# Where half of the MLP's sums of x are made, and by which queue the turned squares travel

## The chip, the cores and the metric

The kernel runs on one core of a Trainium2 chip. The core has a matrix engine (TensorE, PE in the profile, with a second row PEld for loading its stationary operand), a vector engine (VectorE, DVE), a scalar engine (ScalarE, ACT), GpSimd (POOL) and an engine that only issues transfers (SyncE, SP). ACT can issue transfers too; the profile names the queues SPq and ACTq. The metric is the device time of one execution in microseconds.

## The reference

Two residual layers on a sequence of 256 tokens of 2048 features, all in float32. Each layer is a token mixer (stick-breaking attention in the first layer, selected sparse attention in the second) and an MLP:

```python
for i in range(DEPTH):
    h = rms_norm(x, norm_mix[i])
    x = x + mixer(h)                      # ends in o @ w_out
    h = rms_norm(x, norm_mlp[i])
    x = x + jnp.square(jax.nn.relu(h @ w_up[i])) @ w_down[i]
```

`w_up` is 2048 x 8192 and `w_down` 8192 x 2048, so the MLPs hold most of the work.

## The kernel before

**Precision in two parts.** Every product is made from float32 values split into a high part (a copy rounded to the matrix engine's format) and a low part (the value minus the high part). `high` makes `wh` of a weight tile on ACT, `low` makes `wl` on DVE; `xT` holds both parts of the transposed, normalized x. Three products (high by high, high by low, low by high) make one.

**Items.** The whole program is one list of items. An item loads one weight tile of 128 x 1024 (512 KB) and multiplies it; it is given 2.72 us, half that for an item of the seven products below. The main loop at the end goes through the list: for item i it writes `low(i + LEAD)` (LEAD is 3), then `loads`, then `high(i + LEAD + 1)`, perhaps the seeds of an accumulator six items ahead (`before`), then the matmuls of item i and then its `post` functions. `loads` issues, on SP, every weight load for which a buffer is free, for items up to `RAW + 3` = 8 past the one whose `wl` was just written. The tags of the buffers are `wraw` (5) and `sraw` (7 for loads, 2 spare).

**Order.** A scheduler orders each engine's instructions by a timing of its own; what it writes is fixed at build time. `keep_in_program_order` ties an instruction behind the one that was written just before it on the same engine; it can't be put ahead of that one, while others may pass it.

**Sections.** Four sections follow each other: mixer A, MLP, mixer B, MLP. A mixer ends in `out_proj`: 32 items in groups of eight, one group per 512 columns of x, with `add_residual` and `prep` (scaling, transposes, `xT`) behind each group. Each section's `begin` opens a pool of SBUF that is closed when the next section starts.

**The MLP.** The 8192 hidden features are worked through in eight parts f = 0 to 7 of 1024. For f = 0 the product `h @ w_up` is made directly (`up`, 16 items). For f = 1 to 7 (`seven`; a *block* below) it is made by seven products in place of eight quarter products: x is cut in two halves of tokens and two halves of features, and DVE sums quarters of the weights and of x. The sums of x, made once per MLP, are `xS`; `forms` returns its 16 steps, eight for each half b of the feature tiles: two `whole`, four `mixed` and two `parted` (each two copies on ACT and two subtractions on DVE). The steps use scratch in the slot of the second hidden tile `hS` (`draft`) and are made during the `up` items, two at a time (`put(ds, 5, ...)`).

The seven products leave the squared hidden values with tokens on partitions, and the down product wants features there. So at the end of a block come, each at a time after the block's end given by `LAPS` (n = 0 by `LAG` = 2.7 us later than n = 1): `squared` (ACT: relu, square), `turned` (DVE transposes 32 x 32 blocks), `away` (two DMAs to DRAM), `back` (four DMAs from DRAM that finish the transpose) and `parted_h` (high part on ACT, low part on DVE, into `hS`). The DMAs of `away` and `back` are issued by ACT. `back` and the squares take `sraw` slots (`temp`). The last block is turned on PE instead (`turn`).

The items of a block are mixed with 16 items of the down product (`down`: four groups of four items per f), which belong to the part before: `SPAN` says how many go beside the first half of the products, between, and beside the second half; blocks that it does not name take (9, 2, 5). `EARLY` = 5 items of `up` are kept back as the first of these fillers. What is left over follows the last block. A down group ends in `down_done`: two ACT copies of the accumulators to `xs`; the next group is opened by two ACT copies in `seeded`.

Of the kernel before, what the change touches and what calls it, by code (L numbers as in the profile page):

```python
# [8 lines left out]
F32 = mybir.dt.float32  # L9
F32R = mybir.dt.float32r  # L10
# [6 lines left out]
P = 128  # L17
D = 2048
S = 256
# [26 lines left out]
PINNED = 16  # L46
HK = KT // 2
LASTF = 7
SPAN = {1: (7, 2, 5), 2: (8, 2, 5)}
EARLY = 5  # L50
TURNS = (8.0, 10.8)
LAPS = (6.8, 11.5, 18.0, 31.0)
LAG = 2.7
SEED = 6
RAWS = {"wraw": RAW, "sraw": 7}
# [26 lines left out]
def trunk(ctx, tc, x, norm_mix, w_in_a, w_out_a, w_in_b, w_out_b, q_norm_b, k_norm_b, rel_bias,  # L82
# [9 lines left out]
    auxp = ctx.enter_context(tc.tile_pool(name="auxp", bufs=2, space=PSUM))  # L92
    drp = ctx.enter_context(tc.tile_pool(name="drp", bufs=1, space=bass.MemoryType.DRAM))

    opening = tc.tile_pool(name="opening", bufs=1, reuse_waits="tile")
    early = opening.__enter__()

# [103 lines left out]
        dve.tensor_copy(wide["RS"], ps[:, :S])  # L201


    accs = {}

    def rows(w, r0, nr, c0, ncol):
        return w[r0:r0 + nr, c0:c0 + ncol].rearrange("(a p) c -> p a c", p=P)
# [77 lines left out]
    def mlp(l, next_col):  # L285
# [16 lines left out]
        def temp():  # L302
            return sec["pool"].tile([P, WT], F32, name="sraw", bufs=RAWS["sraw"] + SPARE)

        def draft(n):
            if "draft" not in sec:
                sec["draft"] = sec["pool"].tile([P, 4, WT], F32, name="hS", bufs=2)
            return sec["draft"][:, n, :]

        def whole(b, half):  # L310

            t = sec["a", half] = draft(half).rearrange("p (k t) -> p k t", k=4)
            ks = slice(HK * half + 4 * b, HK * half + 4 * b + 4)
            dve.tensor_add(t, xT[:, ks, 0, :].bitcast(F32), xT[:, ks, 1, :].bitcast(F32))

        def mixed(b, n):

            a11, a21 = sec["a", 0][:, :, :P], sec["a", 0][:, :, P:]
            a12, a22 = sec["a", 1][:, :, :P], sec["a", 1][:, :, P:]
            if n % 2 == 0:  # L320
                sec["d", n // 2] = draft(2 + n // 2).rearrange("p (n k t) -> p n k t", n=2, k=4)
            d = lambda m: sec["d", m // 2][:, m % 2]
            if n == 0:
                dve.tensor_sub(d(0), a21, a22)
            elif n == 1:
                dve.tensor_sub(d(1), d(0), a11)
            elif n == 2:
                dve.tensor_sub(d(2), a11, a21)
            else:
                dve.tensor_add(d(3), a12, d(1))  # L330
# [26 lines left out]

        def h_tile(f):
            if f not in sec:
                sec[f] = sec["pool"].tile([P, HK, 2, S], F32R, name="hS", bufs=2)  # L360
            return sec[f]

        def up():
# [6 lines left out]
        def seven(f, c0):  # L370

            g, w = {}, w_up[l]
            quarter = lambda k, t: lambda kt, part: xT[:, HK * k + kt, part, t * P:(t + 1) * P]
            summed = lambda n: lambda kt, part: sec["xS"][:, n, kt, part, :]

            def block(k, n, s, tag):
                return Raw(rows(w, 1024 * k + 256 * s, 256, c0 + 512 * n, 512), KB, 512, tag)

            def item(raws, bank, x, s, source, opens=True):
                def mm(wh, wl):  # L380
# [57 lines left out]
            def se(n):  # L438
                if "se" not in g:
                    g["se"] = sec["pool"].tile([P, 3, 512], F32, name="se", bufs=1)  # L440
                return g["se"][:, n, :]
# [23 lines left out]
            def squared(n):  # L465

                c0, c1 = (se(2), se(1)) if n else (se(0), g["s2"])
                if n:
                    act.activation(c0, c0, AF.Relu)
                act.activation(c1, c1, AF.Relu)  # L470
                for t, c in enumerate((c0, c1)):
                    o = c if f == LASTF else g["sq", n][:, t].rearrange("p (q k b) -> p q b k", q=4, k=4)
                    i = c if f == LASTF else c.rearrange("p (q b k) -> p q b k", q=4, k=4)
                    act.activation(o, i, AF.Square)

            def turn(n, c0, c1):
                h, kts = h_tile(f), slice(4 * n, 4 * n + 4)
                acc = accp.tile([P, 2, 512], F32, name="acc")
                ps = acc.rearrange("p a (k t) -> p (a k) t", k=2)
                for k in range(4):  # L480
                    for t, c in enumerate((c0, c1)):
                        pe.matmul(ps[:, k, t * P:(t + 1) * P], c[:, k * P:(k + 1) * P], ident,
                                  start=k % 2 == 0 and t == 0, stop=k % 2 == 1 and t == 1, is_transpose=True,
                                  skip_group_check=True)
                hi = h[:, kts, 0, :]
                copy(hi, ps)
                dve.tensor_sub(h[:, kts, 1, :], ps, hi.bitcast(F32))
# [10 lines left out]
            def away(n):  # L498
                hd = g["hd", n] = drp.tile([2, P, 512], F32, name="hd", bufs=4)
                for t, c in enumerate((se(2), se(1)) if n else (se(0), g["s2"])):  # L500
                    tc.keep_in_program_order(nc.scalar.dma_start(hd[t], c))

            def back(n):
                hd = g["hd", n].rearrange("t (i b) (q c) -> q b (t i) c", b=32, q=4)
                g["raw", n] = temp().rearrange("p (t c) -> p t c", t=2)
                to = g["raw", n].rearrange("p t (i c) -> p (t i) c", i=4)
                for q in range(4):
                    tc.keep_in_program_order(nc.scalar.dma_start(to[32 * q:32 * q + 32], hd[q]))  # L508

            def parted_h(n):  # L510
                raw = g["raw", n].rearrange("p t (i k a) -> p k (t i) a", i=4, k=4)
# [2 lines left out]
                tc.keep_in_program_order(act.activation(hi, raw, AF.Copy))  # L514
                tc.keep_in_program_order(dve.tensor_sub(lo, raw, hi.bitcast(F32)))

            ends = [(0, after), (1.4, after2), (1.4, lambda: squared(1)), (2.8, lambda: squared(0))]
            if f == LASTF:
                ends += [(TURNS[0], lambda: turn(1, se(2), se(1))), (TURNS[1], lambda: turn(0, se(0), g["s2"]))]
            else:  # L520
                ends.append((0, homes))
                for n in (1, 0):
                    steps = (lambda n=n: turned(n), lambda n=n: away(n), lambda n=n: back(n), lambda n=n: parted_h(n))
                    ends += [(us + (0 if n else LAG), step) for us, step in zip(LAPS, steps)]
                ends.sort(key=lambda e: e[0])
# [50 lines left out]
        def put(items, at, fs, step=1):  # L576
            for n, f in enumerate(fs):
                items[at + n * step].post.append(f)
# [1 line left out]
        ds = up()  # L580
        ds[2 * QA + 1].post.append(stats)
        todo = forms()
        put(ds, 5, [lambda n=n: (todo[2 * n](), todo[2 * n + 1]()) for n in range(8)])
        for f in range(LASTF + 1):
            ds += down(f)
        items, late = ds[:16 - EARLY], []
# [12 lines left out]
        for n, ends in late:  # L599
            at = 0  # L600
            for us, f in ends:
                while at < us:
                    n, at = n + 1, at + items[n + 1].us
                items[n].post.append(f)
        return items, begin


    def mixer_a():
# [3 lines left out]
        def begin(pl):  # L612
            st["pool"] = pl
            st["vs"] = pl.tile([P, 2, D], F32, name="vs", bufs=1)
            st["oT"] = pl.tile([P, HEADS, 2, S], F32R, name="oT", bufs=1)
            st["RSq"] = pl.tile([P, S], F32, name="RSq", bufs=1)
            wide["RS"] = pl.tile([P, S], F32, name="RS", bufs=1)

# [123 lines left out]
    def mixer_b():  # L742
# [3 lines left out]
        def mk(shape, name, dt=F32, bufs=1):  # L746
            return st["pool"].tile(shape, dt, name=name, bufs=bufs)

        def begin(pl):
            st["pool"] = pl  # L750
            st["oT"] = mk([P, HEADS, 2, S], "oT", F32R)
            st["qiT"] = mk([P, 8, S], "w8")
            st["kiT"] = mk([P, S], "kiT")
            wide["RS"] = mk([P, S], "RS")
            st["wi"] = tmp.tile([P, 2, HEADS], F32, name="wi", bufs=1)
            st["sc"] = mk([P, 384], "sc")
            st["mask"] = mk([P, 384], "mask")
            st["kT"] = mk([P, KV, S], "kT")
            st["vh"] = mk([P, 2, 512], "vh", F32R)
            st["vl"] = mk([P, 2, 512], "vl", F32R)  # L760
# [215 lines left out]

    sections = [mixer_a(), mlp(0, 16), mixer_b(), mlp(1, None)]
    items = [it for sec in sections for it in sec[0]]
    first = {}
    n = 0  # L980
    for its, begin in sections:
        first[n] = begin
        n += len(its)
    parts = {}
    queue = []
    for i, it in enumerate(items):
# [68 lines left out]
        if i == 1:  # L1055
            prep(0, 0, False, (1,))
    high(LEAD)
    section, now = None, []
    for i, it in enumerate(items):
        if i in first:  # L1060
            if section is not None:
                section.__exit__(None, None, None)
                if opening is not None:
                    opening.__exit__(None, None, None)
                    opening = None
            section = tc.tile_pool(name=f"section{i}", bufs=1, reuse_waits="tile")
            now[:] = [section.__enter__()]
            first[i](now[0])
        pinned[0] = i < PINNED
        low(i + LEAD)  # L1070
        loads(i + LEAD)
        high(i + LEAD + 1)
        if i + SEED < len(items) and items[i + SEED].before:
            items[i + SEED].before()
        it.mm(*parts.pop(i))
        for f in it.post:
            f()
    section.__exit__(None, None, None)


_INS = ["x", "norm_mix", "w_in_a", "w_out_a", "w_in_b", "w_out_b", "q_norm_b", "k_norm_b", "rel_bias",
# [24 lines left out]
```

## Time and profile before

| | |
|---|---|
| median of 3 runs | 2088.77 us (2087.46, 2095.05, 2088.77) |
| profiled execution | 2094.76 us, of which its span 2093.0 us |
| granted PE clock, mean | 0.994 |
| PE, DVE, ACT busy | 98%, 79%, 65% of the span |
| DMA | 424.05 MB, mean 203 GB/s |
| issued by SP for the weights | 738 loads, nearly all of 512 KB |
| issued by ACT for the squares | 48 `away` of 256 KB, 96 `back` of 128 KB |

The span runs from the first to the last instruction; shares are averages over stages with different limits. Line numbers (L508) are those of the kernel; many operations go through helpers, so that line 107 is every copy on ACT and line 1033 every `wl`. A wait names the engine and line that waited and what it says ended the wait.

### The profile page before, as it was taken

The page shows a single profiled execution, that of the slowest core. Times are in us where ns is not written, and L with a number is a line of the kernel's source. Part 1 is how long each engine was busy: PE and PEld are TensorE (multiplying, and loading weights), DVE is VectorE, ACT ScalarE, POOL GpSimd, SP SyncE. Part 2 cuts the span into 40 slices and gives each one's busy share as a digit, 9 for nine tenths or more (in the row PEclk, how much of TensorE's full clock was granted, in tenths as well). Part 3 has the DMA queues.
Part 4 walks back from the last instruction along what each step waited for, and adds up shares of the span by engine and source line. Part 5 has one row for each costly group of instructions (what it writes and reads, how often), then busy time and mean ns, then how long its engine had stood idle before and what let it go on. Part 6 is the DMA issues. An engine that isn't in the chain of part 4 may idle for free.

```text
span 2093.0 us, 26629 instructions
## 1 busy us (share of the span) xinstructions
PE 2047.4 (98%) x9572; PEld 1700.5 (81%) x9572; DVE 1649.5 (79%) x1745; ACT 1362.6 (65%) x1812; POOL 34.0 (2%) x71
## 2 busy tenths in 40 slices
PE   8999999999899999999999999999989999999999
PEld 7888888887788787787888788888778878778887
DVE  5456665798899998999665877769889999998974
ACT  6445555577677776777764555666767777677774
POOL 0101110000000000000000000000000000000000
PEclk9999999999999999999999999999999999999999
DMA  7666645665766858768566565456575876866844
GB/s 253 193 193 191 176 165 178 192 216 186 235 202 219 252 195 254 210 206 248 163 199 189 157 196 168 151 182 204 185 238 196 250 231 211 258 202 204 260 155 140
DMA packets 274425, 424.05 MB, mean 203 GB/s; under 512 B 16882, under 2 KB 107636, under 8 KB 274292
## 3 DMA queue, kind: packets, MB, share of 16 engines
q1 hardware_dynamic: 233508, 389.74, 58.0%
q10 hardware_dynamic: 40784, 32.61, 5.6%
q8 instruction: 75, 1.23, 0.2%
q14 instruction: 58, 0.48, 0.1%
HBM read 404.41 MB, written 17.82 MB: 202 GB/s over the span
## 4 chain that ended last, share of the span: by engine, by line
PE 88%; DMA 6%; DVE 2%; ACT 2%; issue 1%; ACTq 1%; DVEq 0%; SPq 0%
PE acc L229 47%; PE acc L252 15%; PE acc L387 13%; PE aux L387 9%; DMA sraw<-hd 4%; ACT wh L107 2%; DVE wl L1033 1%; DMA hd<-se 1%; DMA sraw<-in_w_up_dram 1%; PE aux L163 1%; PE aux L229 1%; PE aux L901 1%; DVE sraw L418 0%; ACTq L508 0%; PE acc L637 0%
## 5 line engine op out<-in xcount | busy, mean ns | idle before, releaser
L1033 DVE TENSOR_TENSOR wl<-wraw,wh 128x1024 fp32r<-128x1024 f32 x626 | 756.8, 1219 | 291.0 <-PE acc L229 144.2
L107 ACT ACTIVATE wh<-wraw 128x1024 fp32r<-128x1024 f32 x626 | 650.7, 1057 | 318.5 <-PE acc L229 157.1
L229 PE MATMUL acc<-wh,hS 128*128 128x512 f32 x2016 | 512.2, 392 | 17.6 <-ACT wh L107 14.9
L229 PEld LDWEIGHTS acc<-wh,hS 128*128 128x128 f32 x2016 | 378.5, 189 | 101.0 <-ACT wh L107 19.3
L1033 DVE TENSOR_TENSOR wl<-sraw,wh 128x1024 fp32r<-128x1024 f32 x280 | 337.0, 1219 | 56.0 <-ACT wh L107 41.7
L107 ACT ACTIVATE wh<-sraw 128x1024 fp32r<-128x1024 f32 x280 | 290.4, 1056 | 133.3 <-DVE sraw L425 78.0
L229 PE MATMUL acc<-wl,hS 128*128 128x512 f32 x1008 | 270.2, 389 | 0.0
L252 PE MATMUL acc<-xT,wh 128*128 128x512 f32 x896 | 228.0, 393 | 0.0
L229 PEld LDWEIGHTS acc<-wl,hS 128*128 128x128 f32 x1008 | 189.2, 188 | 39.3
L252 PEld LDWEIGHTS acc<-xT,wh 128*128 128x128 f32 x896 | 160.6, 189 | 28.6 <-ACT wh L107 0.4
L229 PE MATMUL acc<-wh,xT 128*128 128x512 f32 x640 | 165.3, 397 | 0.5 <-ACT wh L107 0.5
L229 PEld LDWEIGHTS acc<-wh,xT 128*128 128x128 f32 x640 | 119.8, 190 | 27.6 <-issue 2.3
L229 PE MATMUL acc<-wh,oT 128*128 128x512 f32 x512 | 133.1, 395 | 0.0
L387 PE MATMUL aux<-wh,xS 128*128 128x512 f32 x448 | 122.2, 394 | 9.7 <-ACT wh L107 9.7
L252 PEld LDWEIGHTS acc<-xT,wl 128*128 128x128 f32 x896 | 123.3, 190 | 9.1
L252 PE MATMUL acc<-xT,wl 128*128 128x256 f32 x896 | 128.6, 283 | 0.0
L387 PE MATMUL acc<-wh,xS 128*128 128x512 f32 x448 | 124.5, 396 | 2.1 <-ACT wh L107 2.1
L107 ACT ACTIVATE xs<-acc 128x512 f32<-128x512 f32 x112 | 60.6, 594 | 97.3 <-PE acc L229 88.7
L387 PE MATMUL acc<-wh,xT 128*128 128x512 f32 x448 | 119.9, 389 | 0.0
L229 PEld LDWEIGHTS acc<-wh,oT 128*128 128x128 f32 x512 | 94.7, 188 | 18.9
L387 PEld LDWEIGHTS aux<-wh,xS 128*128 128x128 f32 x448 | 84.6, 190 | 28.1 <-ACT wh L107 10.9
L387 PEld LDWEIGHTS acc<-wh,xS 128*128 128x128 f32 x448 | 85.8, 193 | 22.3 <-ACT wh L107 4.1
(204 smaller groups left out, 2209.4 us busy)
## 6 DMA issues: line engine op xcount, KB each, us to landing
wraw<-in_w_down_dram SPq DMA_DIRECT2D x256, 512.0 KB, 4.7
sraw<-in_w_up_dram SPq DMA_DIRECT2D x168, 512.0 KB, 5.1
wraw<-in_w_in_a_dram SPq DMA_DIRECT2D x96, 512.0 KB, 3.7
wraw<-in_w_up_dram SPq DMA_DIRECT2D x88, 512.0 KB, 4.4
wraw<-in_w_in_b_dram SPq DMA_DIRECT2D x64, 512.0 KB, 3.7
wraw<-in_w_out_a_dram SPq DMA_DIRECT2D x32, 512.0 KB, 3.5
wraw<-in_w_out_b_dram SPq DMA_DIRECT2D x32, 512.0 KB, 3.9
sraw<-hd ACTq DMA_DIRECT2D x96, 128.0 KB, 7.4
```

What stands on the lines that cost most here:

```text
L107: pin(act.activation(o, i, AF.Copy, scale=scale))
L163: pin(pe.transpose(ps[:, j, t * P:(t + 1) * P], block[t][:, ks], ident))
L229: pin(pe.matmul(acc[t], lhs(k, part, slice(t * P, (t + 1) * P)), w[:, j, :], start=not seed and w is wh and part == 0 and k == 0, stop=w i ...
L252: pe.matmul(acc[:, m, cs], w[:, j, m * P:(m + 1) * P], xT[:, k, xs_, :], start=w is wh and k == 0, stop=w is wl and k == KT - 1)
L387: pe.matmul(acc, x(k, part), w[:, j, :], start=opens and w is wh and part == 0 and k == 0, stop=w is wl and k == HK - 1, **on)
L901: pe.matmul(ps[:, h - lo, :], qT[:, h, t * P:(t + 1) * P], kT[:, n, 0:w], start=True, stop=True)
L1033: pin(dve.tensor_sub(wl, raw, wh.bitcast(F32)))
```

## The change

The change does three things.

1. **Sums.** The two feature halves of x are cut differently (tiles 0 to 3 and 8 to 11 against 4 to 7 and 12 to 15, instead of 0 to 7 against 8 to 15), so that the steps of b = 0 need only the first 1024 columns of x. These eight steps are written behind the last eight items of the preceding output projection, one each; the eight of b = 1 behind `up` items 4 to 11, one each. The scratch comes from `sraw` slots. For this the MLP's pool is opened 13 items into the output projection (`SWAP`), and the attention output `oT` and the hidden tiles `hS` move to a second pool on the right side of SBUF that changes at the old boundary, beside a pad of 120 floats.
2. **Queue.** `away` and `back` are issued by SP.
3. **Times.** `squared` and the homes of its results come later, `LAPS` goes from (6.8, 11.5, 18.0, 31.0) to (9.0, 13.0, 20.0, 29.0), and block 1 gets 15 fillers instead of 14, block 2 16 instead of 15.

```diff
-SPAN = {1: (7, 2, 5), 2: (8, 2, 5)}
+SPAN = {1: (8, 2, 5)}
+SWAP = 13
-LAPS = (6.8, 11.5, 18.0, 31.0)
+LAPS = (9.0, 13.0, 20.0, 29.0)
...
+    edge = ctx.enter_context(tc.tile_pool(name="edge", bufs=1, side="right"))
+    edge.tile([P, 120], F32, name="edge")
...
-            t = sec["a", half] = draft(half).rearrange("p (k t) -> p k t", k=4)
-            ks = slice(HK * half + 4 * b, HK * half + 4 * b + 4)
+            t = sec["a", half] = temp().rearrange("p (k t) -> p k t", k=4)
+            ks = slice(8 * b + 4 * half, 8 * b + 4 * half + 4)
...
-                sec["d", n // 2] = draft(2 + n // 2).rearrange("p (n k t) -> p n k t", n=2, k=4)
+                sec["d", n // 2] = temp().rearrange("p (n k t) -> p n k t", n=2, k=4)
...
-                sec[f] = sec["pool"].tile([P, HK, 2, S], F32R, name="hS", bufs=2)
+                sec[f] = right[0].tile([P, HK, 2, S], F32R, name="hS", bufs=2)
...
-            quarter = lambda k, t: lambda kt, part: xT[:, HK * k + kt, part, t * P:(t + 1) * P]
+            quarter = lambda k, t: lambda kt, part: xT[:, kt // 4 * 8 + 4 * k + kt % 4, part, t * P:(t + 1) * P]
...
-                return Raw(rows(w, 1024 * k + 256 * s, 256, c0 + 512 * n, 512), KB, 512, tag)
+                return Raw(rows(w, 1024 * (s // 2) + 512 * k + 256 * (s % 2), 256, c0 + 512 * n, 512), KB, 512, tag)
...
-                    tc.keep_in_program_order(nc.scalar.dma_start(hd[t], c))
+                    tc.keep_in_program_order(nc.sync.dma_start(hd[t], c))
...
-                    tc.keep_in_program_order(nc.scalar.dma_start(to[32 * q:32 * q + 32], hd[q]))
+                    tc.keep_in_program_order(nc.sync.dma_start(to[32 * q:32 * q + 32], hd[q]))
...
-            ends = [(0, after), (1.4, after2), (1.4, lambda: squared(1)), (2.8, lambda: squared(0))]
+            ends = [(0, after), (1.4, after2)]
             if f == LASTF:
-                ends += [(TURNS[0], lambda: turn(1, se(2), se(1))), (TURNS[1], lambda: turn(0, se(0), g["s2"]))]
+                ends += [(1.4, lambda: squared(1)), (2.8, lambda: squared(0)),
+                         (TURNS[0], lambda: turn(1, se(2), se(1))), (TURNS[1], lambda: turn(0, se(0), g["s2"]))]
             else:
-                ends.append((0, homes))
+                ends += [(3.5, homes), (3.5, lambda: squared(1)), (6.0, lambda: squared(0))]
...
-        put(ds, 5, [lambda n=n: (todo[2 * n](), todo[2 * n + 1]()) for n in range(8)])
+        put(ds, 4, todo[8:])
...
-            st["oT"] = pl.tile([P, HEADS, 2, S], F32R, name="oT", bufs=1)
+            st["oT"] = right[0].tile([P, HEADS, 2, S], F32R, name="oT", bufs=1)
...
+    left, other = {0: sections[0][1]}, {0: None}
     n = 0
-    for its, begin in sections:
-        first[n] = begin
-        n += len(its)
+    for sec, after in zip(sections, sections[1:]):
+        n += len(sec[0])
+        other[n] = None
+        if len(after) == 2:
+            left[n] = after[1]
+            continue
+        wo = n - 4 * QB
+        left[wo + SWAP] = after[1]
+        for k, f in enumerate(after[2]):
+            items[n - len(after[2]) + k].post.append(f)
```

In the main loop the pool on the right side is closed and opened again where an index is in `other`, and the section's pool where it is in `left`.

More of the change, by code (lines that the diff above doesn't have):

```diff
@@ L201, in row_scale_wide @@
         dve.tensor_copy(wide["RS"], ps[:, :S])
-    accs = {}
+    accs, now, right = {}, [], []
     def rows(w, r0, nr, c0, ncol):
@@ L303, in temp @@
             return sec["pool"].tile([P, WT], F32, name="sraw", bufs=RAWS["sraw"] + SPARE)
[L305 to L308, printed above, removed]
         def whole(b, half):
-            t = sec["a", half] = draft(half).rearrange("p (k t) -> p k t", k=4)
-            ks = slice(HK * half + 4 * b, HK * half + 4 * b + 4)
+            t = sec["a", half] = temp().rearrange("p (k t) -> p k t", k=4)
+            ks = slice(8 * b + 4 * half, 8 * b + 4 * half + 4)
             dve.tensor_add(t, xT[:, ks, 0, :].bitcast(F32), xT[:, ks, 1, :].bitcast(F32))
@@ L604, in mlp @@
                 items[n].post.append(f)
-        return items, begin
+        return items, begin, todo[:8]
     def mixer_a():
@@ L750, in begin @@
             st["pool"] = pl
-            st["oT"] = mk([P, HEADS, 2, S], "oT", F32R)
+            st["oT"] = right[0].tile([P, HEADS, 2, S], F32R, name="oT", bufs=1)
             st["qiT"] = mk([P, 8, S], "w8")
@@ L978, in trunk @@
     items = [it for sec in sections for it in sec[0]]
-    first = {}
+    left, other = {0: sections[0][1]}, {0: None}
     n = 0
-    for its, begin in sections:
-        first[n] = begin
-        n += len(its)
+    for sec, after in zip(sections, sections[1:]):
[8 more added lines that the diff above has]
+            items[n - len(after[2]) + k].post.append(f)
     parts = {}
@@ L1057, in trunk @@
     high(LEAD)
-    section, now = None, []
+    section, side = None, None
     for i, it in enumerate(items):
-        if i in first:
+        if i in other:
+            if side is not None:
+                side.__exit__(None, None, None)
+            side = tc.tile_pool(name=f"side{i}", bufs=1, reuse_waits="tile", side="right")
+            right[:] = [side.__enter__()]
+        if i in left:
             if section is not None:
@@ L1067, in trunk @@
             now[:] = [section.__enter__()]
-            first[i](now[0])
+            left[i](now[0])
         pinned[0] = i < PINNED
@@ L1078, in trunk @@
     section.__exit__(None, None, None)
+    side.__exit__(None, None, None)
 _INS = ["x", "norm_mix", "w_in_a", "w_out_a", "w_in_b", "w_out_b", "q_norm_b", "k_norm_b", "rel_bias",
```

## The prediction

> **What bounds the kernel now.** I read the page's busy times first, then TensorE's waits, then the timeline at three of the waits, then the stage table.
>
> ```profile
> span 2093.0 us, 26629 instructions
> ...
> PE 2047.4 (98%) x9572; PEld 1700.5 (81%) x9572; DVE 1649.5 (79%) x1745; ACT 1362.6 (65%) x1812; POOL 34.0 (2%) x71
> ```
>
> PE, the matmuls, is busy for 98% of the span. The change takes no matmul away, so all that it can win is PE's waiting and what that costs in clock. The wait view of PE (total us, count, longest):
>
> ```profile
> PE acc L229 <- ACT wh L107: 15.4, 9, 2.4
> PE aux L387 <- ACT wh L107: 9.7, 2, 4.9
> PE aux L387 <- ACT aux L107: 4.4, 1, 4.4
> ...
> PE acc L229 <- ACT hS L107: 1.9, 1, 1.9
> ```
>
> and the first kind again, in the first 400 us alone:
>
> ```profile
> PE acc L229 <- ACT wh L107: 0.5, 1, 0.5
> ```
>
> So 14.9 us in eight waits of the first kind lie in the MLPs. The timeline says where each kind comes from. Its columns: start, length, engine, line, operation, tiles, count, [idle time before, who ended it]. First ScalarE (ACT) alone, then PE:
>
> ```profile
> 709.57 3.45 ACTq L508 DMA_DIRECT2D sraw<-hd  x3
> 713.07 1.06 ACT L107 ACTIVATE wh<-wraw 128x1024 fp32r<-128x1024 f32 x1 [2.87 <-DMA sraw<-hd]
> ```
> ```profile
> 714.18 2.11 PE L229 MATMUL acc<-wh,hS 128*128 128x512 f32 x8 [2.43 <-ACT wh L107]
> ```
>
> **Issue waits**: ACT stands in three DMA issues of `back` (L508) for 3.45 us, the last of which goes out only when earlier squares have landed. The copy behind them, a `wh` of a weight, needs nothing of those DMAs but is late, and PE waits 2.43 us. I take all eight waits for this kind, one per block from the third on.
>
> ```profile
> 544.16 1.06 ACT L514 ACTIVATE hS<-sraw 128x1024 fp32r<-128x1024 f32 x1 [6.53 <-DMA sraw<-hd]
> ...
> 546.22 2.08 PE L387 MATMUL aux<-wh,xS 128*128 128x512 f32 x4 [4.78 <-ACT wh L107]
> ...
> 555.29 1.22 DVE L515 TENSOR_TENSOR hS<-sraw,hS 128x1024 fp32r<-128x1024 f32 x1
> ```
>
> **Landing waits**: after block 1, ACT comes to `parted_h` (L514) too early and stands 6.53 us until the squares are back; PE waits 4.78 us, and 4.9 in the second MLP.
>
> ```profile
> 473.94 2.07 PE L387 MATMUL aux<-wh,xT 128*128 128x512 f32 x4 [4.35 <-ACT aux L107]
> ```
>
> **The sums**: the copy that opens an accumulator comes late from ACT, and PE waits 4.35 us. The stage table (stretch, its us, busy us and instructions of PE, its weight loads, VectorE (DVE), ACT, POOL, granted clock, DMA share, GB/s) shows whom ACT follows:
>
> ```profile
> 300.00:400.00 100.00, 100.00 (x470) 83.42 (x469) 56.53 (x62) 54.68 (x74) 3.27 (x6) 1.00 0.53 178
> 400.00:440.00 40.00, 40.00 (x226) 34.97 (x225) 40.00 (x57) 27.60 (x43) 0.00 (x0) 1.00 0.68 217
> ```
>
> DVE is busy all 40.00 us while the first block runs beside the sums, but only 56.53 of 100 in the output projection just before. The same table for four-us stretches behind the long waits:
>
> ```profile
> 1546.00:1550.00 4.00, 2.94 (x7) 2.36 (x8) 2.96 (x3) 3.92 (x6) 0.00 (x0) 0.54 0.46 131
> 1550.00:1554.00 4.00, 4.00 (x12) 3.12 (x12) 3.94 (x4) 1.95 (x3) 0.00 (x0) 0.60 0.79 270
> 546.00:550.00 4.00, 3.78 (x10) 3.02 (x11) 3.80 (x4) 3.84 (x5) 0.00 (x0) 0.57 0.48 118
> 474.00:478.00 4.00, 4.00 (x10) 3.13 (x11) 3.37 (x4) 1.49 (x2) 0.00 (x0) 0.50 1.03 379
> ```
>
> PE's busy us times the clock that is missing: 2.94 x 0.46 = 1.4, 4.00 x 0.40 = 1.6, 3.78 x 0.43 = 1.6 and 4.00 x 0.50 = 2.0 us lost.
>
> **What there is to win.** Sums: 4.4 + 2.0 in the first MLP, 1.9 in the second, 8.3 us. Landing waits: 9.7 + 1.6 + 1.4 + 1.6 = 14.3 us. Issue waits: 14.9 us. Together 37.5 us.
>
> **Part 1, the sums.** Half of them (eight steps of sixteen per MLP) go to the last eight items of the output projection.
>
> ```profile
> L337 DVE TENSOR_TENSOR xS<-hS,xS 128x512 fp32r<-128x512 f32 x16 | 10.8, 684 | 0.0
> ...
> L314 DVE TENSOR_TENSOR hS<-xT 128x1024 f32<-128x1024 f32 x8 | 9.6, 1217 | 0.0
> ```
>
> The moved half, per MLP: two `whole` of 1.217 us, and four `mixed` and four `parted` subtractions of the 512-wide form at 0.684, 7.9 us of DVE, and four copies on ACT. PE waited 4.4 us, less than the 7.9 by which DVE gets ahead, so I take all 8.3 us as won. At the new place, eight items of 2.72 us (21.8) take 7.9 us more, where DVE idles 43 of 100: cost zero. If that cover failed (the transposes of the last 512 columns queued behind a step of 1.2 us), six `up` items stand before their use, 16 us. The temporaries move into the nine `sraw` slots, up to four at once beside two of `up_done`; the first block's first items hold two to four loads there. Bounds: nothing, or one late load per MLP (5.1 us to landing). I take nothing. The other pools (squares' side, the 120-float pad, the section swapped after 13 items of the projection) issue nothing; zero, with no row to bound a change of addresses.
>
> **Part 2, the queue.** Per block: 2 x 2 `away` and 2 x 4 `back` leave ACT, twelve issues.
>
> ```profile
> L508 ACTq DMA_DIRECT2D sraw<-hd x96: 309/351/1290, 534.3 to 1966.4; - x96
> ...
> DMA to landing us min/median/max: 2.3/7.4/10.3
> ```
>
> (line 508, `back`: ns of an issue, then us to landing); line 501, `away`:
>
> ```profile
> DMA to landing us min/median/max: 2.0/3.4/5.4
> ```
>
> the weight loads' time to landing, SyncE's (SP's) waits, what ACT waited for weight loads (the view of line 999), and the two DMA queues (packets, MB, share of 16 engines):
>
> ```profile
> sraw<-in_w_up_dram SPq DMA_DIRECT2D x168, 512.0 KB, 5.1
> ```
> ```profile
> SPq L999 <- DVE wl L1033: 1341.5, 542, 11.1
> ...
> SPq L999 <- DMA sraw<-hd: 58.0, 18, 5.9
> ```
> ```profile
>   ACT wh L107: 0.5, 2
> ```
> ```profile
> q1 hardware_dynamic: 233508, 389.74, 58.0%
> q10 hardware_dynamic: 40784, 32.61, 5.6%
> ```
>
> ACT then never stands in an issue: the 14.9 us go. SP takes 12 x 0.35 = 4.2 us more per block, and it idles in waits for `wl` for 1341.5 us of the span. New waits on SP: `away` on `turned`, `back` on `away`'s landing, and behind them stand the weight loads, for which ACT's `wh`, then PE, would wait. By item times (2.72 us, half for the seven products) `away` is written at +13.6 and +16.3 us after the block, `back` at +21.8 and +23.1: 8.2 and 6.8 us for a landing of at most 5.4. So that wait should be short. Further, SP today already waits for a `back` to land 18 times, 58.0 us, up to 5.9 each, and all weight loads together made ACT's `wh` wait 0.5 us. The cushion: a load is written up to eight items ahead, its `wh` one item before its `wl`, which leaves seven items; a block is 28 x 1.36 + 16 x 2.72 = 81.6 us over 44 items, so 13.0 us, minus 5.1 to land: 7.9 us. Cost between 0 and what exceeds it; I take 0.
>
> The landing itself: a packet costs 0.58 x 16 x 2093 / 233508 = 83 ns on the load queue, 0.056 x 16 x 2093 / 40784 = 46 ns on the other. A `back` of 4 x 128 KB in 512-byte rows is 64 packets per DMA engine, 2.9 us alone, yet lands in 7.4; taking turns with load packets would make 64 x (46 + 83) = 8.3. Behind loads on one queue it would be 2.9 plus 1.3 per load ahead (16 packets): about the same, and neither end reaches the 9.5 us between `back` and `parted_h`.
>
> Against this part speaks a rule of the Trainium skill ("DMA: Bandwidth & Descriptors", "Issuing engines are not separate DMA queues"): DMAs of all issuing engines end on the same 16 engines, so another issuer saves only the sequencer's issue time, usually small. By it only the 4.2 us per block would leave ACT, which has slack, and the sum would be that of rival 2. The 3.45 us above, a stand far over three issues of 0.35, speaks against that reading.
>
> **Part 3, the later squares.** `parted_h` is now written behind the last item of a down group (six down and eleven half items, +31.3 us), so on ACT it stands behind that group's two copies to `xs`, which need PE to be there; it can't run early, as at 544.16 it did behind seeds. Squares written at +21.8 have landed by then. The landing waits go: 14.3 us.
>
> But **one wait is added**. With the fillers shifted by one, six down items of the old block remain after a block instead of seven or eight, so the new block's down items begin after six down and thirteen half items, 16.3 + 17.7 = +34.0, where it was seven or eight and sixteen, +40.8 or +43.5. The group's two copies, from the groups of instructions:
>
> ```profile
> L107 ACT ACTIVATE xs<-acc 128x512 f32<-128x512 f32 x112 | 60.6, 594 | 97.3 <-PE acc L229 88.7 <-DMA wraw<-in_w_down_dram 4.2 <-DMA sraw<-hd 4.0
> ```
>
> 31.3 + 2 x 0.59 = 32.5, the high part 1.06 to 33.6 and the low part 1.22 to 34.8 at best (both as at 544.16 and 555.29), while PE asks for it with the second matmul at 34.2: 0.6 us late. After block 1 the low part even started 11.1 us after the high one, but there DVE met an early high part at its own place in the order; now both have one place, so the upper end is two more instructions ahead of it on DVE (1.1 each, back to back), 2.8 us late. Behind it on DVE stand the next `wl`, for which PE waits too. I take 0.8 us, near the lower end, because the instruction order can put a half item in front: 12 x 0.8 = 9.6 us. Ends: 7 and 34.
>
> The tail (22 down items after the last block instead of 24) and the f = 1 stage (15 instead of 14) only move PE work: zero.
>
> **Sum.** 37.5 - 9.6 = 27.9 us less. The profiled execution took 2094.76 us, so 2067 of its like; the median of the runs, 2088.77, is 6 us below it, and gives **2061**.
>
> **The rivals.**
> 1. *The low part becomes the wait.* DVE may well be two instructions behind: 1.8 to 3.1 us each, 22 to 37 us of the 37.5 back, 2073 to 2089, middle 2081. For it: the 11.1 us above. Against: PE's order is made with that lateness known. 0.17.
> 2. *Only the sums help.* PE waits on what ACT waits for, and that is the landing, which no queue changes. For it: 713.07 is put down to `sraw<-hd`. Against: that copy doesn't read it. 2088.8 - 8.3 = 2080. 0.08. The rule of the Trainium skill under part 2 ("DMA: Bandwidth & Descriptors") would give this case.
> 3. *Slower: SP holds the weights.* `back` 1 and `back` 0 now stand 1.3 us apart, eight DMAs in a row, in order with the loads. If SP stands longer than the cushion, each block loses the excess: 12 x (stand - 7.9). It eats the 37.5 us from a stand of 11.0 us; a landing of `away` (5.4) and twice the 2.9 us of `back` make 11.2, and a landing of `away` with the longest one of `back` (10.3) 15.7. Take the middle, 13.4: 66 us, 2117. For it: the stand of 709.57 moves here. Against: the 58.0 and 0.5 us rows. 0.12.
>
> **How the numbers follow.** The forecast has 0.63: from 2051 (all 37.5 won) to 2073. The range, 2050 to 2090, holds it and the first two rivals, 0.88; I count 0.08 of that as lost to the small costs taken as zero, and the third rival lies outside. Half a per cent (10.4 us) is about what a measurement can tell from no change, so faster means under 2078.3: 0.63 and a third of rival 1, 0.68. Same: the rest of it and rival 2, 0.20. Slower: 0.12.
>
> **What would show it.** Part 1 right: DVE clearly under 39 of 40 us early in the MLP, no wait on `aux` of 4 us; wrong: PE waits moved into the projection. Part 2 right: no L508 on ACT's queue, no `wh` idle time ended by `sraw<-hd`; wrong: `wh` waits for weight DMAs. Part 3: waits of `acc` for `hS` L514 or L515, twelve, under 1 us each. The prediction is wrong if these exceed 2 us, or if the weights land late.

## The result, and the profile after

| | before | after |
|---|---|---|
| median, us | 2088.67 (2087.46 to 2095.05, 4 runs) | 2058.84 (2058.55 to 2059.37, 4 runs) |
| profiled execution, us | 2094.76 | 2058.55 |

The ratio is 0.9851, with an interval of 0.9831 to 0.9871: 29.8 us between the medians. The forecast was 2061, 2.2 us above, and the time lies inside its range. But the sum came out for partly wrong reasons, which the runs below take apart.

The page of after, first its span and busy times, then the two queues (packets, MB, share of the 16 engines):

```profile
span 2056.5 us, 26596 instructions
...
PE 2034.7 (99%) x9572; PEld 1694.1 (82%) x9572; DVE 1650.5 (80%) x1745; ACT 1362.0 (66%) x1812; POOL 34.0 (2%) x71
...
q1 hardware_dynamic: 266532, 414.92, 62.6%
q10 hardware_dynamic: 7760, 7.43, 1.2%
```

Against before, the span is 36.5 us shorter: 23.8 of it is idle time of PE (45.6 to 21.8), 12.7 is PE's busy time (2047.4 to 2034.7), though no matmul was taken away. What went from ACT's queue came to SP's, packet for packet: q10 lost 33,024 packets and q1 gained 33,024.

PE's waits after, the small ones of the start-up and the mixer left out:

```profile
PE aux L385 <- ACT wh L110: 10.6, 14, 0.8
...
PE acc L232 <- ACT wh L110: 0.5, 1, 0.5
```

Gone are the eight issue waits, the two landing waits, the `aux` wait of 4.4 us and the `hS` wait of 1.9. New are twelve waits of 0.82 us, one a block (the fourteen hold two more of 0.3). Their size is the one that the forecast gave for a late low part, yet the tile that PE waits for is no `hS` but a weight, `wh`. The timeline of one of them, ACT, then PE, then the first low part on DVE:

```profile
707.39 1.09 ACT L110 ACTIVATE xs<-acc 128x512 f32<-128x512 f32 x2 [1.77 <-PE acc L232]
708.36 1.06 ACT L512 ACTIVATE hS<-sraw 128x1024 fp32r<-128x1024 f32 x1
709.31 1.24 ACT L110 ACTIVATE acc<-xs 128x512 f32<-128x512 f32 x2
710.48 1.04 ACT L110 ACTIVATE wh<-wraw 128x1024 fp32r<-128x1024 f32 x1
711.43 1.04 ACT L512 ACTIVATE hS<-sraw 128x1024 fp32r<-128x1024 f32 x1
```
```profile
710.13 0.61 PE L385 MATMUL aux<-wl,xS 128*128 128x512 f32 x2
711.57 1.19 PE L385 MATMUL aux<-wh,xS 128*128 128x512 f32 x4 [0.82 <-ACT wh L110]
712.60 1.76 PE L232 MATMUL acc<-wh,hS 128*128 128x512 f32 x7
```
```profile
709.99 1.22 DVE L513 TENSOR_TENSOR hS<-sraw,hS 128x1024 fp32r<-128x1024 f32 x1
```

ACT idles 1.77 us until PE has ended a down group, and then has seven copies in a row: two of the accumulators to `xs`, a high part of the turned squares (L512), two into the new accumulators, the `wh`, the other high part. The `wh` is done at 711.52, and PE has been out of work since 710.74. The first low part, which the seven matmuls of `hS` at 712.60 read, is done at 711.21, so it too comes 0.47 us after PE ran out of work: with `hS` PE could not have gone on before that either.

The stage table of after (columns as in the prediction), where the first MLP begins, and the last of these stretches in before:

```profile
300.00:400.00 100.00, 100.00 (x468) 83.36 (x467) 65.33 (x73) 57.08 (x80) 3.27 (x6) 1.00 0.57 189
400.00:440.00 40.00, 40.00 (x226) 34.90 (x225) 33.07 (x46) 25.11 (x39) 0.00 (x0) 1.00 0.59 185
440.00:480.00 40.00, 39.66 (x190) 33.11 (x189) 37.59 (x37) 28.63 (x37) 0.00 (x0) 1.00 0.76 253
```
```profile
440.00:480.00 40.00, 35.40 (x161) 28.91 (x160) 37.43 (x36) 27.75 (x34) 0.00 (x0) 0.91 0.71 238
```

DVE is off its limit early in the MLP (33.07 of 40 where it was 40.00) and does 8.8 us more in the 100 us before. PE's busy time between 440 and 480 rises from 35.40 to 39.66, and the granted clock from 0.91 to 1.00.

SP, which now issues the squares, and what ACT waited for weights:

```profile
698.58 6.78 SPq L506 DMA_DIRECT2D sraw<-hd  x8
```
```profile
ACT wh L110 <- DMA wraw<-in_w_in_a_dram: 1.7, 3, 1.1
...
ACT wh L110 <- DMA wraw<-in_w_down_dram: 1.2, 2, 0.7
```

SP stands 5.9 to 7.7 us in the eight `back` DMAs of a block, and of all weight loads only five came late for ACT's copy, by 2.9 us together.

### The profile page after: what moved, and what is told of

Same layout as the page of the kernel before. It is cut to its first block, busy times and chain, and to the rows that moved or that the text cites. A ratio compares the mean times of both kernels' runs of the same rounds, so it can differ in the third digit from the quotient of the medians.

```text
span 2056.5 us, 26596 instructions
## 1 busy us (share of the span) xinstructions
PE 2034.7 (99%) x9572; PEld 1694.1 (82%) x9572; DVE 1650.5 (80%) x1745; ACT 1362.0 (66%) x1812; POOL 34.0 (2%) x71
## 4 chain that ended last, share of the span: by engine, by line
PE 95%; ACT 3%; DMA 1%; issue 1%; DVE 0%; SPq 0%; ACTq 0%; DVEq 0%
PE acc L232 52%; PE acc L255 15%; PE acc L385 13%; PE aux L385 10%; ACT wh L110 1%; PE aux L166 1%; ACT acc L110 1%; ACT hS L512 1%; PE aux L232 1%; PE aux L900 1%; ACT xs L110 0%; PE acc L636 0%; PE aux L680 0%; PE acc L814 0%; DMA sraw<-hd 0%
## 5 line engine op out<-in xcount | busy, mean ns | idle before, releaser
L385 PE MATMUL acc<-wh,xS 128*128 128x512 f32 x448 | 120.3, 390 | 0.0
```

Source lines behind the costliest of these rows:

```text
L385: pe.matmul(acc, x(k, part), w[:, j, :], start=opens and w is wh and part == 0 and k == 0, stop=w is wl and k == HK - 1, **on)
```

## The experiments

Twelve kernels were run, in three groups of four; each group has runs of its own of before (medians 2092.5, 2093.87 and 2090.91 us), and each ratio is to those. Times of one group can be set side by side, and ratios across groups.

### Each part alone

**sums_only**: before with part 1 alone (steps of b = 0 in the output projection, the others behind `up` items, scratch in `sraw`, second pool).

```diff
-            t = sec["a", half] = draft(half).rearrange("p (k t) -> p k t", k=4)
+            t = sec["a", half] = temp().rearrange("p (k t) -> p k t", k=4)
...
-        put(ds, 5, [lambda n=n: (todo[2 * n](), todo[2 * n + 1]()) for n in range(8)])
+        put(ds, 4, todo[8:])
```

> The kernel before with the sums moved, and nothing else: squares by ACT's queue and at the old times. If the sums were late because DVE had both halves of them beside the first block, the wait of aux for ACT's copy (4.4 us), that for hS in the second MLP (1.9 us) and the lost clock go, 8.3 us: about 2080, and every other wait of PE stays. If the sums matter only together with the other parts, about 2089. If the output projection can't hide them, waits of PE show between 300 and 400 us and the time is 2089 or more.

Measured: 2089.58 us, ratio 0.9989 (0.9976 to 1.0002). Two of PE's waits:

```profile
PE acc L232 <- ACT hS L110: 3.7, 2, 1.9
...
PE acc L232 <- DVE hS L354: 1.5, 2, 0.9
```

The `aux` wait of 4.4 us is gone, and in the first MLP an `hS` wait as in the second has come in its place: `hS` was 1.9 and 0.9 us in all, now it is 3.7 and 1.5. The issue waits (14.8 us) and the landing waits (8.1) stay. Alone, part 1 can't be told from no change: the 8.3 us of the first expectation didn't come.

**queue_only**: before with part 2 alone.

```diff
-                    tc.keep_in_program_order(nc.scalar.dma_start(hd[t], c))
+                    tc.keep_in_program_order(nc.sync.dma_start(hd[t], c))
...
-                    tc.keep_in_program_order(nc.scalar.dma_start(to[32 * q:32 * q + 32], hd[q]))
+                    tc.keep_in_program_order(nc.sync.dma_start(to[32 * q:32 * q + 32], hd[q]))
```

> The kernel before with the squares' transfers on SP's queue, and nothing else. If ACT's standing in the issue of a DMA is the cause of the eight waits, these 14.9 us go and the landing waits after block 1 (4.8 and 4.9 us) stay: about 2074. If ACT waits for the landing itself, whichever queue, all of it stays: 2089. If SP then holds the weights back, over 2099, with waits of ACT's wh for weight loads.

Measured: 2062.85 us, ratio 0.9859 (0.9844 to 0.9875). PE's waits, then ACT after block 1, then how long a `back` (line 508) takes to land:

```profile
PE aux L387 <- ACT aux L107: 4.3, 1, 4.3
...
PE acc L229 <- ACT hS L107: 1.9, 1, 1.9
PE aux L387 <- ACT wh L107: 1.5, 2, 0.7
```
```profile
539.15 1.06 ACT L514 ACTIVATE hS<-sraw 128x1024 fp32r<-128x1024 f32 x1 [3.20 <-DMA sraw<-hd]
```
```profile
DMA to landing us min/median/max: 2.2/3.5/6.1
```

The queue alone gives 29.6 us (2092.5 to 2062.85), nearly all that the whole change gives. It takes the issue waits, as foretold, and most of the landing waits too, which the forecast had left to part 3 and the expectation had left standing: a `back` lands in 3.5 us in place of 7.4, ACT still comes too early to L514 but stands 3.20 us in place of 6.53, and PE's two waits there shrink from 9.7 us to 1.5. The waits of the sums (4.3, 1.9) stay.

**times_only**: before with part 3 alone.

```diff
-SPAN = {1: (7, 2, 5), 2: (8, 2, 5)}
+SPAN = {1: (8, 2, 5)}
...
-LAPS = (6.8, 11.5, 18.0, 31.0)
+LAPS = (9.0, 13.0, 20.0, 29.0)
...
-                ends.append((0, homes))
+                ends += [(3.5, homes), (3.5, lambda: squared(1)), (6.0, lambda: squared(0))]
```

> The kernel before with the later times of the squares and the shifted fillers, and nothing else. If the landing waits came from parted_h running early, they go (14.3 us), the waits of about 0.8 us per block come (about 10 us), and the issue waits stay: about 2085. If the times are what removes the issue waits too, about 2070. If they only work with SP's queue, new issue waits at the new places make it 2089 or more.

Measured: 2085.64 us, ratio 0.9967 (0.9955 to 0.9980). PE's waits:

```profile
PE acc L387 <- ACT wh L107: 9.5, 8, 2.3
PE acc L229 <- DVE hS L515: 7.3, 12, 0.6
PE aux L387 <- DVE wl L1034: 5.9, 11, 0.5
PE acc L229 <- ACT hS L514: 5.2, 11, 0.5
```

Here the waits that the forecast gave for part 3 are there by name, twelve at the low part (L515, 7.3 us), eleven at the high part, with the next `wl` behind them: 18.4 us. So the time of about 2085 that was expected came with other terms than expected. The landing waits are gone, and so is the `aux` wait of 4.4, though the sums are where they were.

**no_sums**: after without part 1 (parts 2 and 3 on before).

```diff
-        put(ds, 4, todo[8:])
+        put(ds, 5, [lambda n=n: (todo[2 * n](), todo[2 * n + 1]()) for n in range(8)])
...
```

> The kernel before with SP's queue and the new times, without the moved sums: what the change is without its first part. If the parts add up, 2059 + 8.3 = 2067, with a wait of PE for the sums' lateness in the first block of each MLP and the twelve waits of 0.8 us as they are. If the earlier sums are also what keeps the later blocks free of waits, over 2075.

Measured: 2057.93 us, ratio 0.9834 (0.9819 to 0.9849), 4.9 us under queue_only in the same group. The twelve waits are there (9.9 us in twelve), no wait of the sums is. So beside the other two parts, part 1 adds nothing: its waits were already gone with part 3. Neither expectation (2067, over 2075) came.

### After with one thing undone or moved

**no_queue**: after with `away` and `back` on ACT again.

```diff
...
-                    tc.keep_in_program_order(nc.sync.dma_start(to[32 * q:32 * q + 32], hd[q]))
+                    tc.keep_in_program_order(nc.scalar.dma_start(to[32 * q:32 * q + 32], hd[q]))
```

> The changed kernel with away and back issued by ACT again. If ACT's standing in the issue is the cost, about 15 us come back, over 1 us per block: 2074, with wh waits ended by sraw<-hd. If the new times alone do away with it, 2059.

Measured: 2087.64 us, ratio 0.9964 (0.9943 to 0.9985). Without the queue the rest of the change is worth 6 us, less than either expectation allowed. What ACT waited for says why:

```profile
ACT wh L110 <- DMA sraw<-hd: 23.9, 10, 4.2
```

Ten times ACT stands behind its own `back` issues before a weight's copy, for 23.9 us. PE's waits show it at two places: 5.8 us for `wh`, and 19.1 for both parts of `hS` and the `wl` behind them, as in times_only. ACT's `back` lands in 4.6 us here (median; 7.4 before), so the later times shorten the landing and not the stand. In after, where SP issues the same DMAs at the same written times, the median is 5.7: at the later times SP's landing is no faster than ACT's.

**no_times**: after with the old times and fillers (parts 1 and 2).

```diff
-SPAN = {1: (8, 2, 5)}
+SPAN = {1: (7, 2, 5), 2: (8, 2, 5)}
...
-LAPS = (9.0, 13.0, 20.0, 29.0)
+LAPS = (6.8, 11.5, 18.0, 31.0)
...
```

> The changed kernel with the old times of the squares and the old fillers. If the landing waits hang on where parted_h stands on ACT, they come back after block 1 (about 14 us with the clock) and the twelve waits of 0.8 us go (10 us): about 2063. If the queue alone had cured them, 2049. If SP's queue needs the later times, 2070 or more.

Measured: 2061.80 us, ratio 0.9850 (0.9818 to 0.9883). The twelve waits are gone, and `hS` waits of 3.7 and 1.8 us are back, as in sums_only. Of the landing waits, which were expected back with 14 us, only 1.7 us are there: the queue alone had cured the rest. By the ratio it can't be told from after: part 3 gives back with its twelve waits about what it takes.

**one_filler_less**: after with 14 fillers beside block 1 again, so that one more down item of the old block remains behind each later block.

```diff
-SPAN = {1: (8, 2, 5)}
+SPAN = {1: (7, 2, 5)}
```

> The changed kernel with one filler less in the first block, so that every later down group begins one item later (seven down items remain after a block, not six). The low part then has 6 us more, about +40 against +35. If the waits of 0.8 us come of it, they go: about 2049. If they come of the order on ACT and of DVE's load in that stretch, they stay, with the same size or a new place: 2056 to 2062. If the first block with 14 fillers is too full for DVE, a wait of several us shows in it.

Measured: 2068.42 us, ratio 0.9879 (0.9841 to 0.9918), above both of the times that were expected. PE's waits, then one of the ten on PE's timeline and the first high part of the same block on ACT's:

```profile
PE acc L385 <- ACT wh L110: 7.5, 10, 0.8
...
PE acc L232 <- ACT hS L110: 3.7, 2, 1.9
PE acc L232 <- DVE hS L354: 1.8, 2, 0.9
```
```profile
695.09 1.20 PE L385 MATMUL acc<-wh,xS 128*128 128x512 f32 x4 [0.74 <-ACT wh L110]
```
```profile
709.44 1.07 ACT L512 ACTIVATE hS<-sraw 128x1024 fp32r<-128x1024 f32 x1 [2.32 <-DMA sraw<-hd]
```

Two things follow. The twelve waits of after are gone here; the ten are others of nearly the same size, for another weight, 12.6 to 14.4 us ahead of the block's first high part (here 695.09 and 709.44). So this run doesn't clear the low part: with more time for it, no wait is left where it is used. And the `hS` waits of the sums are back with 14 fillers: it is the fifteenth down item beside block 1 that took them away, an edit that the prediction costed at nothing.

**earlier_use**: after with the parted squares written at 28.0 us in place of 29.0, one item earlier in the list.

```diff
-LAPS = (9.0, 13.0, 20.0, 29.0)
+LAPS = (9.0, 13.0, 20.0, 28.0)
```

> The changed kernel with parted_h written one half item earlier, ahead of the last item of the down group (28.0 for 29.0). If the twelve waits of 0.8 us come of the low part's lateness, for which another item stands first in PE's order, they shrink: 2049 to 2055. If they come of ACT's order there (the group's copies, the high part, the seeds, then wh) or of DVE being full, they stay or move: 2059. If parted_h then floats ahead of the landing, ACT waits for sraw<-hd and it is over 2065.

Measured: 2044.75 us, ratio 0.9766 (0.9734 to 0.9797), 14.0 us under after by the spans (2042.5 and 2056.5, of different groups). What is left of PE's wait, and ACT at the same place of the program:

```profile
PE aux L385 <- ACT wh L110: 0.7, 2, 0.3
```
```profile
705.25 1.06 ACT L512 ACTIVATE hS<-sraw 128x1024 fp32r<-128x1024 f32 x1 [2.31 <-DMA sraw<-hd]
706.22 1.06 ACT L110 ACTIVATE xs<-acc 128x512 f32<-128x512 f32 x2
707.17 1.06 ACT L512 ACTIVATE hS<-sraw 128x1024 fp32r<-128x1024 f32 x1
708.12 1.24 ACT L110 ACTIVATE acc<-xs 128x512 f32<-128x512 f32 x2
709.29 2.00 ACT L110 ACTIVATE wh<-wraw 128x1024 fp32r<-128x1024 f32 x2
```

All twelve waits are gone. The first high part now goes ahead of the copies to `xs`, into time in which ACT was idle; it waits 2.31 us for its squares, and that costs PE nothing. Both high parts are done before the `wh`, and the first low part, right behind its high part on DVE, is done at 707.58, so that PE has eleven matmuls of `hS` to do before it asks for the `wh`. This version beats both kernels.

### What was still open

**late_low**: earlier_use with the high parts at 28.0 us and the low parts at 29.0 again.

```diff
+LOW = 29.0
...
-                tc.keep_in_program_order(act.activation(hi, raw, AF.Copy))
-                tc.keep_in_program_order(dve.tensor_sub(lo, raw, hi.bitcast(F32)))
+                if low:
+                    tc.keep_in_program_order(dve.tensor_sub(lo, raw, hi.bitcast(F32)))
+                else:
+                    tc.keep_in_program_order(act.activation(hi, raw, AF.Copy))
```

> The best version so far (2044.75) with only the high part of the turned squares at 28.0 us; the low part goes back to 29.0. If the twelve waits of 0.8 us come of ACT's order (the high part standing between the two copies to xs and the next wh), they stay away: 2044 to 2048. If they come of the low part, or of DVE's order around it, they return: 2055 to 2059, with twelve PE waits of about 0.8 us.

Measured: 2044.52 us, ratio 0.9774 (0.9755 to 0.9794). The waits stay away. But the low parts, on DVE, did not move:

```profile
706.84 1.22 DVE L514 TENSOR_TENSOR hS<-sraw,hS 128x1024 fp32r<-128x1024 f32 x1
...
709.11 1.22 DVE L514 TENSOR_TENSOR hS<-sraw,hS 128x1024 fp32r<-128x1024 f32 x1
```

Though written later, they run right behind their high parts, as in earlier_use (706.35 and 708.62; in after 709.99 and 713.39). So the run doesn't take the two apart. Making the turned squares ready earlier clears the twelve waits; whether the high parts' place among ACT's copies or the earlier low parts that follow from it does so stays open.

**earlier_no_sums**: earlier_use without part 1.

```diff
-        put(ds, 4, todo[8:])
+        put(ds, 5, [lambda n=n: (todo[2 * n](), todo[2 * n + 1]()) for n in range(8)])
...
```

> Parts 2 and 3 with the parted squares at 28.0 us in place of 29.0, and without part 1 (the sums of x where they were before). With the old times and the old queue the sums cost an aux wait of 4.4 us and an hS wait of 1.9; beside parts 2 and 3 no such wait was left. If the sums add nothing, the time is that of the best version, 2043 to 2047. If the twelve small waits only covered what the sums win, it is 5 to 8 us above it, 2050 to 2053, with the aux wait or the hS wait back.

Measured: 2044.37 us, ratio 0.9774 (0.9755 to 0.9793), and no wait of the sums. At the best setting found part 1 is worth nothing either.

**pool_queue**: before, `away` and `back` issued by GpSimd.

```diff
...
-                    tc.keep_in_program_order(nc.scalar.dma_start(to[32 * q:32 * q + 32], hd[q]))
+                    tc.keep_in_program_order(nc.gpsimd.dma_start(to[32 * q:32 * q + 32], hd[q]))
```

> The kernel before with away and back issued by GpSimd's queue, nothing else changed. If the gain of part 2 is that ACT no longer stands in an issue, the eight waits of acc L229 for wh go (about 15 us) while the squares land in the 7 us of a row of their own, and the two waits of 4.8 us after block 1 stay: 2070 to 2078. If all of it hangs on the row of the loads, which lands a back in 3.5 us, little is won: 2083 to 2090. If any other issuer does, it is as with SP: 2060 to 2066.

Measured: 2067.0 us, ratio 0.9884 (0.9860 to 0.9908). ACT after block 1, and the landing of a `back`:

```profile
541.14 1.06 ACT L514 ACTIVATE hS<-sraw 128x1024 fp32r<-128x1024 f32 x1 [4.65 <-DMA sraw<-hd]
```
```profile
DMA to landing us min/median/max: 2.6/5.2/8.4
```

All issue waits are gone here too, and the time lies outside the bounds of the first two expectations, near the third. With the same written times, three issuers stand in a row:

| issuer of `back` | lands in, median | ACT stands at L514 | PE's landing waits |
|---|---|---|---|
| ACT (before) | 7.4 us | 6.53 us | 9.7 us |
| GpSimd (pool_queue) | 5.2 us | 4.65 us | 4.7 us |
| SP (queue_only) | 3.5 us | 3.20 us | 1.5 us |

Both other issuers take the issue waits (23.9 us of gain with GpSimd), and with these written times PE's landing waits shrink with the landing. The order of the landings is not one of the queues alone: at the later times it was 4.6 us from ACT (no_queue) and 5.7 from SP (after).

**back_twice**: after, with the first DMA of each `back` issued twice, so that SP must wait for its landing.

```diff
-                for q in range(4):
+                for q in (0, 0, 1, 2, 3):
```

> The kernel after with the first DMA of each back issued twice. The second copy writes the same place, so it can go out only when the first has landed, some 5 us later, twice a block; SP, which now stands 6.8 to 7.9 us in the backs of a block without a loss that PE shows, would stand about 17. By the cushion of the prediction's third rival (7.9 us) each block loses what is above it, some 9 us, twelve times: about 2165, with PE waiting for weight loads. If the cushion is wider, because the loads already issued run for five wraw and up to seven sraw items ahead and a buffer comes free only later, PE waits little and the time stays within some 12 us of the kernel after: 2058 to 2070.

Measured: 2096.07 us, ratio 1.0021 (1.0008 to 1.0034), some 36 us above after by the ratios. SP in one block, then what ACT waited for:

```profile
709.86 8.07 SPq L506 DMA_DIRECT2D sraw<-hd  x6
...
720.08 2.94 SPq L506 DMA_DIRECT2D sraw<-hd  x4
```
```profile
ACT hS L512 <- DMA sraw<-hd: 58.9, 15, 6.4
```

Neither expectation holds. SP did not stand 17 us at a stretch: four of the ten issues went behind further loads, and the two stands were 8.07 and 2.94 us. No MLP weight came late (ACT waited 0.9 us for weight loads, all of them `w_in_a`). What came late were the squares: ACT stood 58.9 us at L512, with the `wh` copies behind it, and PE waited 37.6 us for `wh` in place of 11.1. So the run shows that late squares cost PE through ACT's order; a cushion of 7.9 us for the weights it did not test, since no stretch was clearly longer.

## Why the prediction came out

**What there was to win** was put at 37.5 us; it was at least 49 by the medians. From before to earlier_use the profiled span falls by 50.5 us: PE's waits by 33.7 (its idle time, 45.6 to 11.9) and its busy time by 16.8 (2047.4 to 2030.6). The waits were read rightly (14.9, 9.7, 6.3); the missing term is what follows a wait. Only the lost clock behind the three long waits was counted, 6.6 us in four stretches. Behind the issue waits it was put at nothing, but in before PE's matmuls ran at a lower granted clock behind two of the eight, of 1.93 and 2.08 us:

```profile
798.00:802.00 4.00, 4.00 (x11) 3.17 (x12) 3.48 (x3) 4.00 (x5) 0.00 (x0) 0.60 1.14 256
...
1883.00:1887.00 4.00, 3.77 (x11) 3.01 (x12) 3.50 (x3) 4.00 (x6) 0.00 (x0) 0.66 0.96 257
```

That is 4.00 x 0.40 + 3.77 x 0.34 = 2.9 us more; behind the wait at 714.18, the longest of them (2.43 us), the clock stayed at 1.00, and no run shows what decides. From after to earlier_use twelve waits leave: 9.9 us of waiting and 4.1 us of busy time, 0.34 us more for each.

**Part 1, "all 8.3 us as won": wrong.** Its wait was the right one and went, with DVE's load as foretold (33.07 of 40). But ACT's next late copies, of `hS`, became the wait; the working named no next-late copy for this stall. Alone it measured 0.9989, on top of the others nothing. The cost at the new place was zero as costed: no wait came into the projection.

**Part 2, "the 14.9 us go" at no cost: right; the landing "about the same": wrong.** The stand was read rightly: in the trace's semaphore records, the last DMA of each of the eight stands was held until an earlier `back` with the same completion semaphore (a counter that a transfer raises as it lands) had landed. The one issued at 712.72 waited for the one of 703.85, which landed at 712.69. It did not wait for its own data: the first quarter of the same `back` had gone out at 708.23. The transfers of ACT and SP take turns on eight such semaphores in this trace, those of GpSimd in pool_queue on eight others. The term of the landing was mis-sized: with the old times it was 3.5 us where 7.4 stood, so this part took most of the landing waits as well and gave 29.6 us. Taking turns with the loads packet by packet was the estimate for the old queue and 1.3 us per load ahead for the new; neither is shown by a run. Why GpSimd's landing lies between isn't settled, nor why at the later times ACT's landed in 4.6 us and SP's in 5.7: the queue is not all of it.

The rule of the Trainium skill that was weighed there ("DMA: Bandwidth & Descriptors", "Issuing engines are not separate DMA queues") leaves only the issue time to be won by another issuer. The runs of this case don't agree: two other issuers gained 23.9 and 29.6 us.

**Part 3: 14.3 won, 9.6 lost.** The wait of 0.8 us a block, twelve times, came as priced, but for another tile: PE waits for a `wh` behind ACT's copies at the change of group. The low part is late there too, by 0.47 us, behind the half item that PE's order puts in front of it, and that had been allowed for. By the name that was foretold the wait was found only with ACT as the issuer (times_only and no_queue), where it grew to 18.4 us with what stood behind it. The landing waits that the part was credited with were, but for 1.5 us, already won by part 2. What it won besides were the waits of the sums, 6.3 us: the `hS` wait through the fifteenth filler of block 1, which the prediction set to zero; whether the `aux` wait went with the filler or with the later squares was not taken apart, but in before it lies at 473.94, 41 us ahead of the first squaring (514.9), which speaks for the filler.

**The sum** of 27.9 us stands beside 29.8 measured by luck, because the errors met: the sums' waits were credited to the wrong part, the landing waits too, and each was counted once. The rest is the choice of the median: against the profiled execution the sum gave 2067 (2094.76 - 27.9), 8 us above the 2058.55 measured. Of that, 6.1 us is PE's busy time (12.7 less against the 6.6 counted), the time behind the waits; the rest is mainly small waits that went and were not counted. That execution of before lay 6 us above its median, so that the error doesn't show in the 2061.

**The rivals.** The first (low part two instructions behind, 22 to 37 us) did not come: the twelve waits were 0.82 us each, and the low part was 0.47 us late, not 1.8 to 3.1. The second (only the sums help) is refuted by sums_only and queue_only, which show the reverse. The third (SP holds the weights) did not come: SP stood 5.9 to 7.7 us, below the 11.0 from which it was to decide, and waited there for `away` 28.6 us in all, 2.1 at most. Whether a stand of 11 us would cost what was said stays open.

## What to carry to other kernels

A DMA that may have to wait before it can go out doesn't belong in the queue of an engine whose copies feed the bound engine: here its stand, not the 0.35 us of its issue, was the price. When a wait is struck from the list, look for the next late copy on the same engine before counting it as won, and test each part alone: two of three parts here overlapped, and the third added nothing. When a run is to take two causes apart, look in its trace whether the edit moved what it was to move: in late_low it didn't. Where an engine idles just ahead of a burst of copies that all gate the bound engine, move into that idle time whatever may go early, even if it has to wait there.

## What the hardware showed beside this

`away` and `back` together are 33,024 packets when ACT or SP issues them, and far fewer from GpSimd, whose row in the page of pool_queue is:

```profile
q0 software_dynamic: 8448, 25.18, 3.8%
```

With a quarter of the packets, a `back` did not land faster than from SP (5.2 against 3.5 us). And a short wait of PE costs more than it lasts: four matmuls that take 1.07 us elsewhere take 1.19 behind the wait at 711.57 with the clock granted in full (1.00 from 712 to 716). That is 0.12 of the 0.34 us. Another 0.16 is overlap: a pair of matmuls like the one at 710.13 takes 0.61 us, and elsewhere the next one starts 0.45 us after it (704.92 and 705.37), but behind a wait nothing overlaps. The last 0.06 was not found.
